# HGRN2 and short-convolution decoder step: 42 of 80 input projections as seven-product 2x2 block matrices, with stage results kept in DRAM

## The chip, the cores and the metric

The kernel runs on one core of one Trainium2 chip. The metric is the device time of one execution in microseconds (us); a smaller time is better. The engines are TensorE (PE, with its weight loads shown apart as PEld), VectorE (DVE), ScalarE (ACT), GpSimd (POOL) and SyncE (SP), which issues all the DMAs here.

## The reference

One decoder layer for 1040 prompt tokens (16 learned meta tokens, then 1024) and 8 single-token samples, width 1024, all in float32:

```python
xn = rmsnorm(h, norm_pre)
proj = xn @ w_in                         # 1024 x 10240: ten sections of 1024 channels
q, fr, i_in, z_a, b_g, c_g, h_c, z_b, gate_a, gate_b = split(proj)
f = lb + (1 - lb) * sigmoid(fr);  k = 1 - f;  qa = silu(q)
o = gated linear recurrence over (qa, k, i_in, log f), 8 heads of 128 x 128   # branch A
y_a = (rmsnorm(o) * silu(z_a)) @ w_a
u = c_g * h_c                                                                # branch B
y_b = (b_g * conv3(u) * silu(z_b)) @ w_b
out = (sigmoid(gate_a) * y_a + sigmoid(gate_b) * y_b) @ w_o
h = h + rmsnorm(out, norm_post)
```

The states of the recurrence and the last two rows of u are outputs too.

## The kernel before

**Layout.** Activations lie channel-major: 128 channels on the partitions, 1048 columns (NX) along the free dimension: even prompt chunks, odd prompt chunks back to front, 8 sample columns, 16 meta columns. The first 1032 (NY) have an output. The normalised input is eight such blocks, each split exactly into a high and a low float32r part (`xh`, `xl`), which stay in SBUF (tag `xn`) to the end.

**A section** is one block of 128 output channels of a projection. `weight` (L76) loads its 1024 x 128 weights (512 KB, line 79) and `split` (L89 to 92) makes the two parts: ACT casts the high part (L91), DVE subtracts it (L92). `gemm` (L94 to 105) then makes three matmuls for each of eight blocks k: high by high, high by low, low by high.

```python
94      def gemm(w, xh, xl, n0, n):
96          wh, wl = w
97          pt = gbank()
98          for k in range(8):
99              ks = slice(128 * k, 128 * k + 128)
100             pe.matmul(pt[:, 0:n], wh[:, ks], xh[k][:, n0:n0 + n], start=(k == 0), stop=False)
101             pe.matmul(pt[:, 0:n], wh[:, ks], xl[k][:, n0:n0 + n], start=False, stop=False)
102             pe.matmul(pt[:, 0:n], wl[:, ks], xh[k][:, n0:n0 + n], start=False, stop=(k == 7))
```

`section` (L107) runs it over three chunks of columns, 512, 256 and 264 to 280 wide (CH_Y, CH_C, CH_M, L127 to 129), 72 matmuls in all, and a function of the caller takes each chunk out of PSUM. There are 80 sections on the input (`w_sec`, eight for each of the ten parts of `proj`) and 16 on the outputs of the two branches (`w_a`, `w_b`).

**Order.** Head 0's four sections run by groups of columns while the input is still being normalised. For each of seven heads, `weave` (L531) puts the four sections of the next head (`projections`, L202) between the steps of one head's recurrence (`hgrn`, L209). Head 7's recurrence lies between four sections of gate A (L565). Then come the other gates A and y_a (L568), branch B (L588 to 634: for each m the sections 5, 6, 4 and 7, with u, the convolution and the products on DVE, ACT and POOL between them), gate B and y_b (L672 to 676, L717), and the output projection (L761), 512 columns to a matmul. The outputs of the branches and `merged` stay in SBUF (tag `z`, eight slots).

**What sets the order of the queues.** The tile framework fixes each engine's order when the program is built: by its own model of time it takes the first instruction in program order whose inputs and slots are ready. So a queue is not in program order (a weight cast is taken one section ahead), but on the chip each engine keeps to the order that was fixed. A tag has as many slots as its `bufs`; a new tile waits until the last reader of its slot is done. PSUM has four banks `g` and four banks `h`.

Of the kernel before, what the change touches and what calls it, by code (L numbers as in the profile page):

```python
# [19 lines left out]
NX = 1048  # L20
NY = 1032
# [9 lines left out]
def hybrid_step(ctx: ExitStack, tc: tile.TileContext,  # L31
# [41 lines left out]
    def small(n, tag="st", bufs=6):  # L73
        return sb.tile([128, n], F32, name=tag, tag=tag, bufs=bufs)

    def weight(src, raw=None, hi=None, lo=None, eng=None):  # L76
        """128 output channels of a [1024, *] weight: exact float32r parts [128, 8, 128]."""
        raw = slot(raw or "wr", 1024)
        sync.dma_start(raw.rearrange("p (k c) -> p k c", k=8), src.rearrange("(k p) c -> p k c", p=128))
        hi = slot(hi, 1024, F32R) if hi else slot("wh", 1024, F32R, 2)  # L80
        lo = slot(lo, 1024, F32R) if lo else slot("wl", 1024, F32R, 2)
        split(raw[:, 0:1024], hi[:, 0:1024], lo[:, 0:1024], eng)
        return hi, lo

    def w_sec(sec, m, *tags, eng=None):
        c0 = 1024 * sec + 128 * m
        return weight(w_in[0][:, c0:c0 + 128], *tags, eng=eng)
# [713 lines left out]
```

## Time and profile before

| what | value |
|---|---|
| runs | 1364.84 us median of 3 (1364.76 to 1364.93) |
| profiled execution, first to last instruction (span) | 1363.2 us |
| time of a run outside the span, by the median | 1.6 us |
| PE busy | 1341.0 us, 98% of the span, 8705 matmuls |
| DVE, ACT, POOL busy | 637.5, 347.8, 97.9 us |
| moved by DMA | 82.96 MB, 61 GB/s on average |

The profiled execution has no time of its own beside its span; the 1.6 us are the median of the runs less the span. Matmuls are pipelined, so the duration of one is longer than the distance to the next; what a matmul costs is read from the distance between starts.

### The profile page before, as it was taken

What the parts mean: (1) busy time and instruction counts of PE and PEld (TensorE: products, weight loads), DVE (VectorE), ACT (ScalarE), POOL (GpSimd) and SP (SyncE); (2) the same over time, 40 slices, a digit from 0 to 9 for tenths busy, and PEclk for the clock granted to TensorE, in tenths of its full rate; (3) what the DMA queues carried; (4) which work ended last, traced back from release to release, by engine and by line L of the source; (5) the groups of instructions that cost most, each with busy time, mean ns of one, the idle gap of its engine ahead of it and who ended that gap; (6) DMA issues with size and microseconds to landing.
All of it is one profiled execution on the core that took longest, in us unless ns stands there. A gap on an engine that the chain in (4) does not pass through costs nothing.

```text
span 1363.2 us, 20362 instructions
## 1 busy us (share of the span) xinstructions
PE 1341.0 (98%) x8705; PEld 1207.5 (89%) x8705; DVE 637.5 (47%) x1049; ACT 347.8 (26%) x702; POOL 97.9 (7%) x200
## 2 busy tenths in 40 slices
PE   6999999999999999999999999999999999999998
PEld 6989898989898999999999999999999999998786
DVE  5497676676767677521122333333333322216422
ACT  7233232323232333301111221122112211115211
POOL 5002010110101020100000000000000000000000
PEclk9999999999999999999999999999999999999999
DMA  7021312121221212111111111111111111123321
GB/s 235 19 63 50 87 33 86 34 78 50 63 78 51 62 49 63 34 47 47 47 47 47 47 47 47 47 47 47 47 47 47 49 47 47 47 62 110 112 98 70
DMA packets 125316, 82.96 MB, mean 61 GB/s; under 512 B 2911, under 2 KB 118728, under 8 KB 125226
## 3 DMA queue, kind: packets, MB, share of 16 engines
q1 hardware_dynamic: 125226, 81.67, 20.1%
q8 instruction: 68, 1.11, 0.3%
q14 instruction: 22, 0.18, 0.0%
HBM read 72.57 MB, written 9.05 MB: 60 GB/s over the span
## 4 chain that ended last, share of the span: by engine, by line
PE 91%; DVE 6%; DMA 1%; issue 1%; ACT 0%; POOL 0%; SPq 0%; DVEq 0%; POOLq 0%; ACTq 0%
PE g L100 25%; PE g L101 25%; PE g L102 25%; PE h L339 2%; PE g L771 2%; PE g L769 2%; PE g L770 2%; DVE a L347 2%; PE h L405 1%; PE h L404 1%; PE h L387 1%; DMA wr<-in_w_in_dram 1%; DVE x L342 1%; PE h L419 1%; PE h L370 1%
## 5 line engine op out<-in xcount | busy, mean ns | idle before, releaser
L100 PE MATMUL g<-xn,wh 128*128 128x256 f32 (+4 forms) x1888 | 613.3, 325 | 0.0
L101 PE MATMUL g<-xn,wh 128*128 128x256 f32 (+4 forms) x1888 | 603.6, 320 | 0.0
L102 PE MATMUL g<-xn,wl 128*128 128x256 f32 (+4 forms) x1888 | 603.5, 320 | 0.1
L100 PEld LDWEIGHTS g<-xn,wh 128*128 128x128 f32 x1888 | 356.8, 189 | 29.3 <-issue 1.6
L102 PEld LDWEIGHTS g<-xn,wl 128*128 128x128 f32 x1888 | 355.6, 188 | 27.5 <-DVE wl L92 0.5
L101 PEld LDWEIGHTS g<-xn,wh 128*128 128x128 f32 x1888 | 356.0, 189 | 26.6 <-DVE xn L92 0.2
L92 DVE TENSOR_TENSOR wl<-wr,wh 128x1024 fp32r<-128x1024 f32 x92 | 112.3, 1221 | 203.5 <-ACT wh L91 203.4
L91 ACT CAST wh<-wr 128x1024 fp32r<-128x1024 f32 x93 | 97.7, 1050 | 392.8 <-PE g L101 387.0
L347 DVE COPY_PREDICATED a<-masks,h 128x512 f32<-128x512 uint8 x56 | 59.4, 1061 | 4.3 <-PE h L335 4.1
L339 PE MATMUL h<-x,u 128*128 128x128 f32 x384 | 52.4, 279 | 4.5 <-DVE x L342 3.9
L339 PEld LDWEIGHTS h<-x,u 128*128 128x128 f32 x384 | 48.0, 191 | 8.3 <-issue 3.3
L337 ACT COPY u<-k 128x512 f32<-128x512 f32 x48 | 30.4, 632 | 90.5 <-DVE k L341 44.1
L597 DVE TENSOR_TENSOR u<-g,c 128x256 f32<-128x256 f32 (+2 forms) x32 | 12.9, 425 | 64.9 <-PE g L102 64.9
L557 DVE TENSOR_TENSOR z<-g,z 128x512 f32<-128x512 f32 (+2 forms) x24 | 12.4, 517 | 63.7 <-PE g L102 63.7
L342 DVE TENSOR_TENSOR x<-x,ee 128x512 f32<-128x512 f32 x48 | 33.0, 688 | 15.9 <-PE h L339 15.1
L743 DVE TENSOR_TENSOR z<-g,t 128x512 f32<-128x512 f32 x16 | 11.1, 691 | 57.0 <-ACT cs L742 57.0
L341 DVE TENSOR_TENSOR k<-k,ee 128x512 f32<-128x512 f32 x48 | 33.0, 688 | 4.8 <-ACT u L337 4.8
L621 DVE TENSOR_TENSOR t<-g,t 128x512 f32<-128x512 f32 (+2 forms) x24 | 12.4, 516 | 42.8 <-PE g L102 42.8
L101 PE MATMUL g<-zs,wh 128*128 128x512 f32 (+2 forms) x96 | 30.8, 321 | 0.0
L100 PE MATMUL g<-x,wh 128*128 128x512 f32 (+2 forms) x96 | 30.8, 320 | 0.0
L102 PE MATMUL g<-x,wl 128*128 128x512 f32 (+2 forms) x96 | 30.6, 319 | 0.0
L742 ACT ACTIVATE cs<-g 128x512 f32<-128x512 f32 x16 | 9.6, 597 | 74.8 <-PE g L771 45.4
(324 smaller groups left out, 1805.5 us busy)
## 6 DMA issues: line engine op xcount, KB each, us to landing
wr<-in_w_in_dram SPq DMA_DIRECT2D x77, 512.0 KB
z<-in_x_prompt_dram SPq DMA_DIRECT2D x8, 512.0 KB
sin<-in_state_hgrn_dram SPq DMA_DIRECT2D x8, 512.0 KB
vb<-vd SPq DMA_DIRECT2D x8, 512.0 KB
out_dram<-sin SPq DMA_DIRECT2D x8, 512.0 KB
wr<-in_w_a_dram SPq DMA_DIRECT2D x8, 512.0 KB
wr<-in_w_b_dram SPq DMA_DIRECT2D x8, 512.0 KB
out_dram<-z SPq DMA_DIRECT2D x16, 256.0 KB
```

The costliest lines, as they stand in the source:

```text
L91: act.copy(hi, src)
L92: (eng or vec).tensor_tensor(out=lo, in0=src, in1=hi.bitcast(F32), op=ALU.subtract)
L100: pe.matmul(pt[:, 0:n], wh[:, ks], xh[k][:, n0:n0 + n], start=(k == 0), stop=False)
L101: pe.matmul(pt[:, 0:n], wh[:, ks], xl[k][:, n0:n0 + n], start=False, stop=False)
L102: pe.matmul(pt[:, 0:n], wl[:, ks], xh[k][:, n0:n0 + n], start=False, stop=(k == 7))
L337: act.copy(comp(kms, ko, nb, B, B), kc)
L339: pe.matmul(pt[:, 128 * j:128 * j + 128], kms[:, ko + 128 * j:ko + 128 * j + 128], comp(X, 128 * j + B, nb // 4, 512 - B, B), start=True, ...
L341: vec.tensor_tensor(out=kc, in0=kc, in1=cap(eb, eo + 1, [[2, nb], [512 // B - 1, 2], [0, B]]), op=ALU.mult)
L342: vec.tensor_tensor(out=xc, in0=xc, in1=cap(eb, eo, [[2, nb], [512 // B + 1, 2], [0, B]]), op=ALU.mult)
L347: vec.copy_predicated(comp(A, B, nb, 512 - B, B), bass.AP(masks[:].tensor, masks[:].offset + 512 * l, ap=[list(masks[:].ap[0]), [2 * B, nb ...
L769: pe.matmul(pt, gh[k][:, ts], woh[k][:, hs], start=(k == 0), stop=False)
L770: pe.matmul(pt, gh[k][:, ts], wol[k][:, hs], start=False, stop=False)
```

## The change

The two halves of the columns are laid out alike, 524 wide (HL; 516, HY, have an output), and every chunk of a section is now 256 or 260 to 268 columns wide, four chunks for three. 38 of the sections on the input (all of the recurrence, gate A for m = 0 to 5) stay as they were otherwise. The other 42 (sections 5, 6, 4, 7 of branch B, gate A for 6 and 7, gate B) are taken in 21 pairs. A pair is a 2 x 2 block product (two blocks of output channels, two halves of the 1024 input channels, two halves of the columns), made by the seven products of Strassen's method in Winograd's form.

`block_sums` makes the four sums of the activations once: POOL adds the parts back together, DVE takes the differences, ACT and DVE split them. `strassen` makes four sums of weights for each pair on POOL and splits seven operands. The partial sums that more than one result needs are copied out of PSUM between products (`held`, slots `sc`, two of them). The outputs of the branches and the gates are stored to DRAM (`oz_d`, `ob_d`, `ga_d`, `gb_d`) and loaded again. The gates are all made before y_a and y_b. y_a, y_b and the first four blocks of the output projection take k as the outer loop. POOL takes part of branch B's products.

```diff
-    CH_M = ((0, 512), (512, 256), (768, 280))     # all columns
-    CH_Y = ((0, 512), (512, 256), (768, 264))     # prompt, sample
+    def halves(n):
+        return tuple((h, c0, w) for h in range(2) for c0, w in ((0, 256), (256, n - 256)))
+    CH_M = halves(HL)
+    CH_Y = halves(HY)
...
+    BUFS = {"x": 2, "f": 2, "k": 2, "zs": 2, "z": 2, "w": 6, "wr": 4, "cs": 2, "sc": 2, "st": 5}
...
     def run_hgrn(m):
+        Z = slot("z", NY)
         yield from hgrn(m, tiles[m], Z)
+        sync.dma_start(oz_d[m], Z)
...
-    weave(gates_first(), 24, run_hgrn(7), N_HG)
+    weave(gates_plain(0, 1, 2, 3), 32, run_hgrn(7), N_HG)
...
+    def block_sums():
+        for k in range(4):
+            ta, tb = (slot(t, 2 * HL) for t in (("kt", "s"), ("a", "ee"))[k % 2])
+            (r12, r22), (r11, r21) = ((t[:, 0:HL], t[:, HL:2 * HL]) for t in (ta, tb))
+            for r, b in ((r12, (0, 1)), (r11, (0, 0)), (r22, (1, 1)), (r21, (1, 0))):
+                h, l = in_block(blk[b])(k)
+                pool.tensor_tensor(out=r, in0=h.bitcast(F32), in1=l.bitcast(F32), op=ALU.add)
+            yield
+            d1 = t1_raw(k)
+            vec.tensor_tensor(out=d1, in0=r12, in1=r11, op=ALU.subtract)
+            vec.tensor_tensor(out=r12, in0=r22, in1=r12, op=ALU.subtract)
+            vec.tensor_tensor(out=r22, in0=r22, in1=d1, op=ALU.subtract)
+            split(r22, *in_quarters(t2)(k))
+            yield
+            vec.tensor_tensor(out=r21, in0=r21, in1=r22, op=ALU.subtract)
+            split(r12, *in_quarters(t3)(k))
+            yield
+            split(r21, *in_quarters(t4)(k))
+            yield
+
+    weave(gates_plain(4, 5), 16, block_sums(), 16)
+    bt = (slot("b01h", 4 * HL, F32R), slot("b01l", 4 * HL, F32R))
+    for k in range(4):
+        split(t1_raw(k), *in_block(bt)(k))
+    sets = [in_block(blk[0, 0]), in_block(blk[1, 0]), in_quarters(t2), in_block(bt), in_quarters(t3), in_quarters(t4),
+            in_block(blk[1, 1])]
...
+        def add(p):
+            if p < len(pairs):
+                sa, sb_ = (slot(t, 1024) for t in (("kt", "s"), ("a", "ee"))[p % 2])
+                s1, s2, s3, s4 = sums[p] = sa[:, 0:512], sa[:, 512:1024], sb_[:, 0:512], sb_[:, 512:1024]
+                pool.tensor_tensor(out=s1, in0=quad(p, 1, 0), in1=quad(p, 1, 1), op=ALU.add)
+                pool.tensor_tensor(out=s2, in0=s1, in1=quad(p, 0, 0), op=ALU.subtract)
+                pool.tensor_tensor(out=s3, in0=quad(p, 0, 0), in1=quad(p, 1, 0), op=ALU.subtract)
+                pool.tensor_tensor(out=s4, in0=quad(p, 0, 1), in1=s2, op=ALU.subtract)
+        def operand(i):
+            p, j = divmod(i, 7)
+            if p < len(pairs):
+                s1, s2, s3, s4 = sums[p]
+                src = (quad(p, 0, 0), quad(p, 0, 1), s2, s1, s3, quad(p, 1, 1), s4)[j]
+                w = ops[i] = slot("w", 1024, F32R)
+                split(src, w[:, 0:512], w[:, 512:1024])
...
+        for p, (_, chunks, evac, end) in enumerate(pairs):
+            b1, b2 = (gbank, hbank) if p % 2 == 0 else (hbank, gbank)
+            pa, pb, pc = ([b() for _ in chunks] for b in (b1, b2, b1))
+            for j in range(7):
+                i = 7 * p + j
+                if j == 0 and p:
+                    load(p + 1)
+                if j == 1:
+                    add(p + 1)
+                operand(i + 3)
+                w = ops.pop(i)
+                dst = (pa, pb, pa, pc, pa, pa, pc)[j]
+                for (c0, n), pt in zip(chunks, dst):
+                    for k in range(4):
+                        xh, xl = sets[j](k)
+                        mm3(pt[:, 0:n], w[:, 128 * k:128 * k + 128], w[:, 512 + 128 * k:640 + 128 * k],
+                            xh[:, c0:c0 + n], xl[:, c0:c0 + n], j in (0, 1, 3) and k == 0, k == 3,
+                            j not in (0, 1, 3))
+                if j in (0, 2, 4):
+                    sc = slot("sc", HL)
+                    for (c0, n), pt in zip(chunks, pa):
+                        act.copy(sc[:, c0:c0 + n], pt[:, 0:n])
+                    held[j] = sc
+                if j in (1, 4, 5, 6):
+                    r, h, banks, s = {1: (0, 0, pb, 0), 4: (1, 1, pc, 4), 5: (1, 0, pa, None), 6: (0, 1, pc, 2)}[j]
+                    for (c0, n), pt in zip(chunks, banks):
+                        evac(r, h, c0, n, pt[:, 0:n], None if s is None else held[s][:, c0:c0 + n])
+                if p == len(pairs) - 1 and j in tail:
+                    tail[j]()
+            end()
...
+    def b_pair(m):
+        def evac(r, h, c0, n, pt, s):
+            t = conv[m][:, HY * h + c0:HY * h + c0 + n]
+            if s is not None:
+                vec.tensor_tensor(out=s, in0=pt, in1=s, op=ALU.add)
+            y = pt if s is None else s
+            if r == 0:
+                (vec if h else pool).tensor_tensor(out=t, in0=t, in1=y, op=ALU.mult)
+            else:
+                sg = slot("cs", 512)[:, 0:n]
+                act.activation(out=sg, in_=y, func=AF.Sigmoid)
+                (pool if h else vec).tensor_tensor(out=sg, in0=y, in1=sg, op=ALU.mult)
+                vec.tensor_tensor(out=t, in0=t, in1=sg, op=ALU.mult)
+        return (sec_of(4, m), sec_of(7, m)), ((0, 256), (256, 260)), evac, lambda: sync.dma_start(ob_d[m], conv[m])
...
+    pairs = [f(m) for m in range(8) for f in (u_pair, b_pair)]
+    pairs.append(gate_pair(8, 6, ga_d))
+    pairs += [gate_pair(9, m, gb_d) for m in (0, 2, 4, 6)]
+    strassen(pairs, sets, tail)
...
+        for k in range(8):
+            ks = slice(128 * k, 128 * k + 128)
+            xh, xl = parts[k]
+            for (h, c0, n), pt in zip(CH_Y, banks):
+                o = HY * h + c0
+                mm3(pt[:, 0:n], wh[:, ks], wl[:, ks], xh[:, o:o + n], xl[:, o:o + n], k == 0, k == 7)
```

Of the parts left out: `mm3` is the three matmuls of `gemm`. `u_pair` takes sections 5 and 6 with chunks of 256 and 262 columns; its results of the first channel block go to C by a DVE add, those of the second are multiplied with C into u, for the first half of the columns on DVE and for the second on POOL (two instructions of 256 columns and a small one). At its end stand six small POOL copies, then for each half one ACT instruction and two DVE instructions of the convolution, 512 columns each, and three small ones on DVE. `gate_pair` ends in a sigmoid on ACT and two stores of 528 KB. `tail` loads branch A's output back and splits it into the slots of activation blocks that the last pair no longer reads.

## Rows read from the trace of the kernel before

**Rows 1.** The page: busy time of each engine, and PE, PEclk and GB/s by slices.

```profile
PE 1341.0 (98%) x8705; PEld 1207.5 (89%) x8705; DVE 637.5 (47%) x1049; ACT 347.8 (26%) x702; POOL 97.9 (7%) x200
...
PE   6999999999999999999999999999999999999998
...
PEclk9999999999999999999999999999999999999999
...
GB/s 235 19 63 50 87 33 86 34 78 50 63 78 51 62 49 63 34 47 47 47 47 47 47 47 47 47 47 47 47 47 47 49 47 47 47 62 110 112 98 70
```

**Rows 2.** The page: the chain that ended last, by engine.

```profile
PE 91%; DVE 6%; DMA 1%; issue 1%; ACT 0%; POOL 0%; SPq 0%; DVEq 0%; POOLq 0%; ACTq 0%
```

**Rows 3.** Windows: a head, branch B, the merge, 256-column matmuls alone.

```profile
core 0: us, PE busy (x) PEld busy (x) DVE busy (x) ACT busy (x) POOL busy (x), PEclk, DMA share, GB/s
...
260.00:400.00 140.00, 139.13 (x964) 126.75 (x963) 94.28 (x157) 43.52 (x101) 16.67 (x28) 1.00 0.20 58
...
960.00:1060.00 100.00, 100.00 (x631) 90.35 (x631) 36.99 (x64) 21.41 (x33) 2.12 (x14) 1.00 0.17 48
...
1160.00:1260.00 100.00, 99.91 (x640) 90.09 (x639) 36.96 (x57) 28.56 (x48) 0.00 (x0) 1.00 0.25 75
...
32.00:45.00 13.00, 13.00 (x110) 12.82 (x109) 6.62 (x12) 2.40 (x6) 1.70 (x2) 1.00 0.03 8
```

**Rows 4.** Timeline, PE: start, duration, line. First matmul of consecutive chunks in branch B.

```profile
778.47 0.28 PE L100 MATMUL g<-xn,wh 128*128 128x266 f32 x1
...
781.43 0.40 PE L100 MATMUL g<-xn,wh 128*128 128x512 f32 x1
...
787.03 0.28 PE L100 MATMUL g<-xn,wh 128*128 128x256 f32 x1
...
789.85 0.28 PE L100 MATMUL g<-xn,wh 128*128 128x264 f32 x1
...
792.78 0.40 PE L100 MATMUL g<-xn,wh 128*128 128x512 f32 x1
```

**Rows 5.** Groups by form, ACT: count, busy us, mean ns.

```profile
L91 ACT CAST c<-u 128x512 fp32r<-128x512 f32 x8 | 4.9, 613 | 4.2 <-DVE u L241 4.2
...
L590 ACT COPY c<-g 128x256 f32<-128x256 f32 x8 | 3.0, 372 | 17.9 <-PE g L102 17.9
```

**Rows 6.** The same view, DVE.

```profile
L613 DVE SCALAR_TENSOR_TENSOR t<-u,vecs,t 128x512 f32<-128x512 f32 x16 | 11.3, 746 | 0.0
...
L597 DVE TENSOR_TENSOR u<-g,c 128x256 f32<-128x256 f32 x16 | 6.8, 425 | 37.4 <-PE g L102 37.4
...
L92 DVE TENSOR_TENSOR c<-u,c 128x512 fp32r<-128x512 f32 x8 | 5.4, 677 | 0.0
```

**Rows 7.** Timeline, start of the kernel, POOL: a 1024-column subtraction.

```profile
13.64 2.38 POOL L92 TENSOR_TENSOR wl<-c,wh 128x1024 fp32r<-128x1024 f32 x1
```

**Rows 8.** The same stretch, DVE.

```profile
14.74 1.31 DVE L462 TENSOR_TENSOR lbt<-vecs 128x8 f32<-128x8 f32 x1
16.08 0.17 DVE L463 TENSOR_TENSOR lbt<-vecs,lbt 128x8 f32<-128x8 f32 x1
```

**Rows 9.** Timeline of a head, DVE and POOL.

```profile
166.25 0.67 DVE L341 TENSOR_TENSOR k<-k,ee 128x512 f32<-128x512 f32 x1
166.28 1.85 POOL L263 TENSOR_TENSOR k<-k,f 128x8 f32<-128x8 f32 x1
166.85 1.21 DVE L92 TENSOR_TENSOR wl<-wr,wh 128x1024 fp32r<-128x1024 f32 x1
168.21 0.76 POOL L263 TENSOR_TENSOR k<-k,em 128x8 f32<-128x8 f32 x3
```

**Rows 10.** Timeline, DVE: the end of head 7, and y_a's first chunk.

```profile
571.41 1.23 DVE L92 TENSOR_TENSOR s<-z,kt 128x1032 fp32r<-128x1032 f32 x1 [2.70 <-PE h L405]
...
582.20 0.69 DVE L557 TENSOR_TENSOR z<-g,z 128x512 f32<-128x512 f32 x1 [2.52 <-PE g L102]
```

**Rows 11.** The chain that ended last: wait for one 512 KB weight load.

```profile
62.85 3.60 DMA wr<-in_w_in_dram
```

More of the change, by code (lines that the diff above doesn't have):

```diff
@@ L15 @@
 EPS = 1e-6
-NX = 1048
-NY = 1032
+HL = 524
+HY = 516
+NX = 2 * HL
+NY = 2 * HY
 def cap(t, off, dims):
@@ L71, in rsqrt, with small @@
         pool.tensor_tensor(out=out, in0=out, in1=half[0:rows, 0:n], op=ALU.pow)
[L73 to L87, printed above, removed]
+    def small(n):
+        return slot("st", n)
     def split(src, hi, lo, eng=None):
@@ L565, in hybrid_step, with gate_plain @@
-    weave(gates_first(), 24, run_hgrn(7), N_HG)
-    for m in range(4, 8):
-        oz_parts(m)
-    for m in range(8):
-        if m >= 4:
-            drain(gate_a(m))
-        drain(y_a(m))
+        weave(projections(m + 1, tiles), 32, run_hgrn(m), N_HG, 1 if m else 2)
+    def gate_plain(m):
+        G = slot("z", NY)
+        yield from section(w_sec(8, m), CH_Y, lambda h, c0, n, pt: act.activation(
+            out=G[:, HY * h + c0:HY * h + c0 + n], in_=pt, func=AF.Sigmoid))
+        sync.dma_start(ga_d[m], G)
@@ new lines, in gate_pair, with evac, end @@
+    def gate_pair(sec, m, dst):
+        G = []
+        def evac(r, h, c0, n, pt, s):
+            if not G:
+                G.extend(slot("z", NY) for _ in range(2))
+            if s is not None:
+                vec.tensor_tensor(out=s, in0=pt, in1=s, op=ALU.add)
+            act.activation(out=G[r][:, HY * h + c0:HY * h + c0 + n], in_=pt if s is None else s, func=AF.Sigmoid)
+        def end():
+            for r in range(2):
+                sync.dma_start(dst[m + r], G[r])
+        return (sec_of(sec, m), sec_of(sec, m + 1)), ((0, 256), (256, 260)), evac, end
@@ new lines, in fill @@
+    def fill(src, parts, ks, places):
+        raws = {}
+        for k in ks:
+            raws[k] = slot(("c", "u", "t")[k % 3], NY)
+            sync.dma_start(raws[k], src[k])
+        his, los = places
+        for k, hi, lo in zip(ks, his, los):
+            split(raws[k][:, 0:NY], hi, lo)
+            parts[k] = hi, lo
+    pa, pb = {}, {}
+    one = lambda *tags: [place(t, 1)[0] for t in tags]
+    tail = {0: lambda: fill(oz_d, pa, (0, 1), (place("b00h", 2), place("b00l", 2))),
+            1: lambda: fill(oz_d, pa, (2, 3), (place("b10h", 2), place("b10l", 2))),
+            2: lambda: fill(oz_d, pa, (4, 5), (one("x", "k"), one("f", "zs"))),
+            3: lambda: fill(oz_d, pa, (6, 7), (place("b01h", 2), place("b01l", 2)))}
@@ L646, in w_bm, with gate_in, w_am @@
+    def gate_in(src, m):
+        g = slot("z", NY)
+        sync.dma_start(g, src[m])
+        return g
+    def w_am(m):
+        return weight(w_a[0][:, 128 * m:128 * m + 128])
     def w_bm(m):
         return weight(w_b[0][:, 128 * m:128 * m + 128])
[L649 to L658 removed]
@@ new lines, in hybrid_step, with ev @@
+    for m in range(8):
+        w, g = wb, gb
+        if m < 7:
+            wb, gb = w_bm(m + 1), gate_in(gb_d, m + 1)
+        def ev(ys, pt):
+            vec.tensor_tensor(out=g[:, ys], in0=pt, in1=g[:, ys], op=ALU.mult)
+            vec.tensor_tensor(out=merged[m][:, ys], in0=merged[m][:, ys], in1=g[:, ys], op=ALU.add)
+        y_gemm(w, pb, ev)
+        if m == 2:
+            out_weight(0, *one("x", "f"))
+            out_weight(1, *one("k", "zs"))
+        if m == 4:
+            (h2, h3), (l2, l3) = place("b01h", 2), place("b01l", 2)
+            out_weight(2, h2, l2)
+            out_weight(3, h3, l3)
+        if m == 5:
+            merged_parts(0, *one("c", "u"))
```

551 lines of the change are left out of this document (290 added, 261 removed).

## Prediction

> **What bounds the kernel now.** I read the page first, then the chain, the windows, and the starts of single matmuls. TensorE is busy in 98% of the span and, but for the first and the last slice, in all slices at nine tenths or more, at full granted clock [rows 1]. The chain that ended last is 91% PE [rows 2]. By stages: inside the heads PE is idle for 0.87 of 140 us, in branch B for nothing, in the merge for 0.09 of 100 us [rows 3]. So time goes only where matmul time goes, and stays only where nothing new makes PE wait. In branch B DVE is busy 37% of the time, ACT 21%, POOL 2%: there is room beside PE, but a change that fills it must be checked for waits.
>
> What a matmul costs is the distance between starts: a chunk of 24 takes 5.60 us at 512 columns, 2.82 us at 256, 2.93 us at 264, 2.96 us at 266 [rows 4], which is 233, 117.5, 122 and 123 ns. A matmul of 256 columns thus costs half of one of 512; per further column it costs (122 - 117.5)/8, some 0.55 ns, so that I take 120 ns for 260 columns, 121 for 262 and 124 for 268.
>
> **Part 1, seven products for eight.** A pair before is two sections. Of branch B's sections 5 and 6: 2 x (5.60 + 2.82 + 2.96) = 22.8 us; of all the others: 2 x (5.60 + 2.82 + 2.93) = 22.7 us. A pair after is 7 products x 4 blocks k x 3 matmuls = 84 matmuls on each of two chunks: 84 x (0.1175 + 0.121) = 20.0 us, and 84 x (0.1175 + 0.120) = 19.95 us. One product is a seventh, 2.86 us. The gain is 8 x 2.75 + 13 x 2.75 = **58 us**, all of it on the path.
>
> Does a stream of 256-column matmuls alone keep this pace? In the stretch from 32 to 45 us there is nearly nothing else, and 110 records in 13 us are one in 118 ns [rows 3]. The Trainium skill (TensorE: Matmul & The Clock Gate, section Back-to-back issue gap) speaks against the change here: it has streams of weight load and matmul sustain 131 ns at 512 columns and 81 ns at 128, so that fewer columns save far less than in proportion. An estimate on the line between these two is 98 ns at 256; by it a pair would go from 48 x (131 + 98 + 98) ns = 15.7 us to 168 x 98 ns = 16.5 us, and the change would lose 17 us instead of gaining 58. The trace does not agree: 233 and 117.5 ns.
>
> **Part 2, four chunks for three.** The plain sections and y_a, y_b: 24 x (0.1175 + 0.120) x 2 = 11.40 us against 11.35; for 28 sections of heads 1 to 7, 6 of gate A and 16 of y_a and y_b that is **+2 us**. Head 0 had four chunks before.
>
> **Part 3, the sums of the activations.** Here I expect a stall. POOL's price is not shown at this size: 2.38 us for 1024 columns [rows 7] makes 1.19 for 512 and 1.22 for 524. A DVE subtraction of 512 with both inputs in SBUF takes 0.677 us [rows 6], 0.69 for 524. These two do not run side by side: while POOL's 2.38 us instruction ran, a DVE instruction on 8 columns, 0.17 us otherwise, took 1.31 us and ended with it [rows 7, 8]; and POOL's 0.2 us instruction took 1.85 us behind two DVE instructions one right after the other, to the end of the second [rows 9]. So the times add: `block_sums` has 16 POOL adds, 19.5 us, and 4 x (4 + 3) DVE instructions, 19.3 us. POOL can begin when head 7's slots come free, at 571.4 [rows 10], and ends the first four adds near 576.3. Three rounds of 4.9 + 4.8 us follow, to 605.4, then 3.4 us (four DVE instructions and a cast) until the last quarter of the third product's operand: 608.8. PE's cover: gates 0 to 3 end at 582.2 - 5.6 = 576.6 (y_a's first chunk is taken out at 582.2 [rows 10]), gates 4 and 5 take 22.8 us, the first two products need no sum, 5.7 us: 605.1. The stall is some 4 us, and about 4 more because POOL's sums for the first pairs and the split of the fourth operand (4 x 0.69 us) compete for the same time: **8 us**. Bounds: 0 if the order that is built lets the sums begin earlier, 15 if no product goes ahead of them: 605.4 + 4.8 + 2.8 + 1.3 for a first operand, against 599.4.
>
> **Part 4, the work beside a pair.** Of a u pair in its 20 us: POOL 4 sums at 1.19, two products at 0.6, a small one and six copies at 0.25 [rows 9]: 7.7 us. DVE with two SBUF inputs: 7 x 0.677 + 4 x 0.746 + three small, 8.3 us; these two exclude each other, 16 of 20 us. DVE's instructions on PSUM add 8 x 0.425 = 3.4 us [rows 6]. ACT: 7 casts at 0.613, 6 copies at 0.372 [rows 5], two of 512 at about 0.61: 7.8 us. A b pair has 7.2 and 7.3 us in place of 7.7 and 8.3. So each engine fits behind PE, the shared path at 80%. Waits by place: the operands are made up to five products ahead (six slots `w`), 14 us, which covers any queue seen here. The copies of `pa` must be done before the next product onto `pa`; after the first and third product another lies between (2.86 us), after the fifth only the half product of the other chunk, 1.43 us, against a cast that may be in front and the copy, 0.613 + 0.372. The DVE adds on `pc` have 2.86 us, against one POOL sum that may be in front, a split and two adds: 1.19 + 0.677 + 2 x 0.425 = 2.7. Both just fit. A trace of these waits does not exist; bounds are 0 and one late instruction (a POOL sum, 1.2 us) at each of the two tight places in 21 pairs, 50 us. I take 0.3 us per pair, **6 us**, near the low end, since each place has its cover even with one instruction in front.
>
> SP: a b pair's store of 528 KB waits for the last product, some 2 us into the next pair, and two loads of 512 KB are queued behind it. One load takes 3.6 us and more [rows 11]; 1.55 MB at the 235 GB/s of the first slice [rows 1] are 6.6 us. They land near 9 us, and the first cast from them is needed at the latest at 11 us if it is taken three products ahead: nothing on the path. The y stages move 1.04 MB in 11.4 us, 91 GB/s, less than the 112 of the last slices.
>
> **Part 5, the rest.** In the heads each section has one more evacuation, each head two more POOL instructions and one more small DMA: PE covers them, idle 0.6% there. If that cover were gone, an evacuation would cost its 0.37 us. Two `z` slots for eight make a gate wait for the store of the one before the last; four PSUM banks, 2.85 us of matmuls each, stand before that. The splits of branch A's output fall in the last pair, 8 x 1.2 us of DVE in 20, where no next operands are made. The merge and the output projection keep their matmuls. Together **+4 us**, between 0 and 10.
>
> **Sum.** 1363.2 - 58 + 2 + 8 + 6 + 4 = 1325.2 us of span, and with the 1.6 us outside it (median 1364.84 less 1363.2) **1327 us**.
>
> **The rivals.** (a) *No stalls*: the order that is built hides parts 3 to 5. For it: PE's 98% now. 1363.2 - 58 + 2 + 1.6 = 1309 us. (b) *POOL and DVE hold up PE*: the two exclude each other and 80% is near the limit, so evacuations come late. Part 3 at 15 us, parts 4 and 5 at 20 and 8: 1352 us. For it: POOL waited through two DVE instructions, alike in six of the eight heads [rows 9]; against it: five products of lead. (c) *Slower: the copies of partial sums come late on ScalarE.* Place: `held` before products three, five and six of a pair. ACT keeps to an order fixed in advance; if a sigmoid or a cast in front of the copy waits for a DVE instruction that waits for POOL (1.2 + 0.7 us), PE stops each time. It decides from (58 - 2 - 8 - 4)/21 = 2.1 us per pair; at 1.2 us in each of three places, 3.6 us per pair, the time is 1327 - 6 + 76 = 1397 us. For it: three waits of PE that were not there before, in each pair; against it: ACT has 12 of 20 us free. (d) *Seven products save nothing*: 256-column matmuls met one after another for 400 us cost 133 ns instead of 117.5, or the stalls happen to equal the gain: within 2.7 us of 1365. Only the stretch of 13 us speaks on it, and against it.
>
> **How the numbers follow.** Forecast 0.48, (a) 0.17, (b) 0.16, (c) 0.15, (d) 0.04. About 0.2% is what a measurement of this kernel can tell from no change. Forecast, (a) and (b) are faster, 0.81; (d) is the same, 0.04; (c) is slower, 0.15. The range of the forecast itself is 1313 to 1345 (its unknown terms from some 4 to 36 us); the range for eight in ten takes in (a) at its lower end and (b) with 8 us to spare at its upper, 1309 to 1360, and leaves out (c) and (d).
>
> **What would show it.** Chunks of 24 matmuls at 256 columns still 2.82 us; a pair some 20 us from start to start, with PE idle below 0.5 us in it; one gap of PE of 5 to 10 us behind gate A's sixth section, ended by DVE or ACT; DVE subtractions stretched to over 1 us wherever POOL's sums run. I would be wrong if pairs are 21.5 us or longer, with PE waiting for ACT's copies or DVE's adds, if the gap behind the gates is 15 us, or if heads or y stages, where I expect nothing, become longer by more than 1%.

## The result, and the profile after

| | before | after |
|---|---|---|
| median of the runs | 1364.88 us (1364.76 to 1365.02, 4 runs) | 1324.52 us (1323.37 to 1328.36, 4 runs) |
| profiled execution, span | 1363.2 us | 1322.1 us (the run: 1323.88) |
| PE busy | 1341.0 us, 8705 matmuls | 1293.5 us, 10409 matmuls |
| DVE, ACT, POOL busy | 637.5, 347.8, 97.9 us | 771.5, 433.0, 295.2 us |
| bytes moved | 82.96 MB | 117.07 MB |

The ratio of the times is 0.971, with a 95% interval of 0.9695 to 0.9723: faster by 40 us. The forecast was 1327 us.

The page of the kernel after: the busy times, PE by slices, and the chain by engine, which answer to [rows 1, 2].

```profile
PE 1293.5 (98%) x10409; PEld 1259.5 (95%) x10409; DVE 771.5 (58%) x1336; ACT 433.0 (33%) x959; POOL 295.2 (22%) x372
...
PE   6999999999999999998999999999999999999997
...
PE 90%; DVE 6%; POOL 1%; DMA 1%; ACT 1%; issue 1%; SPq 0%; DVEq 0%; POOLq 0%; ACTq 0%
```

PE is still what bounds the kernel. One new slice in the middle has an 8: it lies near 600 us, where the pairs begin. The windows answer to [rows 3]. The columns are the window, its length, the busy time and number of instructions of PE, PEld, DVE, ACT and POOL, then the granted clock, the DMA share and GB/s. First come 5 us near the start of the pairs, then a u pair, a b pair, and 100 us of pairs.

```profile
609.00:614.00 5.00, 3.97 (x21) 3.97 (x21) 5.00 (x6) 3.55 (x8) 3.05 (x3) 0.66 0.36 105
...
652.37:672.56 20.19, 20.19 (x170) 20.19 (x169) 10.37 (x23) 6.30 (x13) 6.97 (x7) 1.00 0.27 80
672.56:692.55 19.99, 19.99 (x170) 19.99 (x169) 12.95 (x23) 8.81 (x19) 10.99 (x13) 1.00 0.18 54
...
700.00:800.00 100.00, 100.00 (x837) 100.00 (x837) 60.12 (x109) 37.64 (x79) 44.54 (x53) 1.00 0.22 64
```

**A pair in the steady state has no wait at all.** PE is busy for 20.19 of 20.19 us and for 19.99 of 19.99. The starts of the first matmul of each of the 21 pairs, taken from PE's timeline, lie 28.16 us apart at the first pair, 21.01 at the second, 20.19 (u pairs) or 19.97 to 20.00 (b and gate pairs) at the next 18, and 21.49 from the last pair to the first matmul of y_a. The timeline of PE in one u pair, first matmul of consecutive chunks, answers to [rows 4]:

```profile
772.92 0.28 PE L109 MATMUL g<-b00h,w 128*128 128x256 f32 x1
...
774.34 0.28 PE L109 MATMUL g<-b00h,w 128*128 128x262 f32 x1
...
775.79 0.28 PE L109 MATMUL h<-b10h,w 128*128 128x256 f32 x1
...
777.20 0.28 PE L109 MATMUL h<-b10h,w 128*128 128x262 f32 x1
```

Twelve matmuls take 1.42 us at 256 columns and 1.45 us at 262, that is 118 and 121 ns each, for 117.5 and 121 forecast.

**What the start of the pairs costs.** The timeline of PE at the first pair:

```profile
604.61 0.28 PE L111 MATMUL g<-b00h,w 128*128 128x256 f32 x1
610.03 0.58 PE L109 MATMUL g<-b00h,w 128*128 128x262 f32 x1 [5.15 <-ACT z L564]
610.42 0.42 PE L110 MATMUL g<-b00l,w 128*128 128x262 f32 x1
...
612.60 0.42 PE L111 MATMUL g<-b00h,w 128*128 128x262 f32 x1
...
613.52 0.29 PE L110 MATMUL h<-b10l,w 128*128 128x256 f32 x1
```

PE stands still for 5.15 us, until ACT has taken gate 5's second chunk (a sigmoid) out of the bank that the second half of product one needs. Then the eleven matmuls from 610.42 to 612.60 start 0.218 us apart, where the same shape takes 0.121 elsewhere. The granted clock of the 5 us from 609 is 0.66 on average, so PE ran at its lower level of 1.2 GHz for most of them; some 15 matmuls at 0.1 us more are 1.5 us. The Trainium skill (TensorE: Matmul & The Clock Gate, section Back-to-back issue gap) gives columns divided by 1.2 as the gap in ns of a single matmul at the lower clock. An estimate by this formula for 262 columns is 218 ns, and the trace agrees.

Why was the sigmoid late? ACT's timeline, then DVE's and POOL's, in the same stretch:

```profile
591.24 0.39 ACT L564 ACTIVATE z<-g 128x260 f32<-128x260 f32 x1 [2.48 <-PE g L111]
600.93 1.17 ACT L85 CAST f<-kt 128x524 fp32r<-128x524 f32 x2 [9.31 <-DVE kt L597]
...
606.83 0.62 ACT L85 CAST w<-kt 128x512 fp32r<-128x512 f32 x1 [3.76 <-POOL kt L629]
...
609.07 0.63 ACT L85 CAST f<-a 128x524 fp32r<-128x524 f32 x1 [0.56 <-DVE a L597]
609.60 0.38 ACT L564 ACTIVATE z<-g 128x260 f32<-128x260 f32 x1
```

```profile
580.36 0.69 DVE L595 TENSOR_TENSOR c<-kt,s 128x524 f32<-128x524 f32 x1
...
592.17 1.79 DVE L595 TENSOR_TENSOR u<-kt,s 128x524 f32<-128x524 f32 x1 [3.74 <-POOL s L592]
593.89 1.80 DVE L86 TENSOR_TENSOR sin<-ee,it 128x524 fp32r<-128x524 f32 x1
...
607.27 1.76 DVE L597 TENSOR_TENSOR a<-a,u 128x524 f32<-128x524 f32 x1
```

```profile
586.04 3.56 POOL L592 TENSOR_TENSOR kt<-b01h,b01l 128x524 f32<-128x524 f32 x1 [7.95 <-DVE k L86]
589.56 1.31 POOL L592 TENSOR_TENSOR kt<-b11h,b11l 128x524 f32<-128x524 f32 x1
...
595.09 1.77 POOL L592 TENSOR_TENSOR a<-b11h,b11l 128x524 f32<-128x524 f32 x1
596.83 1.78 POOL L592 TENSOR_TENSOR ee<-b00h,b00l 128x524 f32<-128x524 f32 x1
```

The sigmoid at 609.60 stands in ACT's fixed order behind casts that wait: one of the block sums for 9.31 us for DVE, one of the first pair's weight sums for 3.76 us for POOL, and the last one, at 609.07, for the difference that DVE ends at 609.03. DVE and POOL take turns from 592 to 600 us, when POOL adds the block sums, and again from 603.9 us on, when it makes the weight sums (L628 to 631) of the first pair. A DVE instruction that takes 0.69 us alone is on record for 1.8 us, a POOL add that takes 1.31 us alone for 1.77; one of each starts every 1.72 us, a little less than the 2.0 us that the two would take one after the other. The Trainium skill (SBUF — State Buffer, section SBUF: two separate sides) calls this an exclusive lock between a GpSimd instruction and a VectorE instruction with two SBUF inputs; taking turns in the trace agrees with it. Two waits for slots come before that: DVE's first difference waits for the slot of head 7's output until 580.36, and POOL waits 7.95 us for a slot that DVE's splits have to free.

### The profile page after: what moved, and what is told of

The parts are those of the page before. It is cut to its first block, busy times and chain, and to the rows that moved or that the text cites. A ratio compares the mean times of both kernels' runs of the same rounds, so it can differ in the third digit from the quotient of the medians.

```text
span 1322.1 us, 24885 instructions
## 1 busy us (share of the span) xinstructions
PE 1293.5 (98%) x10409; PEld 1259.5 (95%) x10409; DVE 771.5 (58%) x1336; ACT 433.0 (33%) x959; POOL 295.2 (22%) x372
## 2 busy tenths in 40 slices
DMA packets 134590, 117.07 MB, mean 89 GB/s; under 512 B 3953, under 2 KB 119770, under 8 KB 134478
## 4 chain that ended last, share of the span: by engine, by line
PE 90%; DVE 6%; POOL 1%; DMA 1%; ACT 1%; issue 1%; SPq 0%; DVEq 0%; POOLq 0%; ACTq 0%
PE g L109 19%; PE g L110 18%; PE g L111 18%; PE h L111 8%; PE h L110 8%; PE h L109 8%; PE h L366 3%; PE h L433 1%; PE h L431 1%; PE h L414 1%; DVE w L86 1%; PE h L171 1%; PE h L447 1%; PE h L397 1%; DMA it<-in_x_prompt_dram 0%
## 5 line engine op out<-in xcount | busy, mean ns | idle before, releaser
L86 DVE TENSOR_TENSOR w<-wr,w 128x512 fp32r<-128x512 f32 (+1 forms) x114 | 127.0, 1115 | 58.5 <-ACT w L85 58.5
L109 PE MATMUL g<-b00h,w 128*128 128x256 f32 (+1 forms) x448 | 131.8, 296 | 5.5 <-ACT z L564 5.1
L110 PE MATMUL g<-b00l,w 128*128 128x256 f32 (+1 forms) x448 | 128.2, 286 | 0.0
L111 PE MATMUL g<-b00h,w 128*128 128x256 f32 (+1 forms) x448 | 128.0, 286 | 0.0
L109 PE MATMUL g<-b10h,w 128*128 128x256 f32 (+2 forms) x440 | 125.8, 286 | 0.0
L110 PE MATMUL g<-b10l,w 128*128 128x256 f32 (+2 forms) x440 | 124.7, 283 | 0.0
L111 PE MATMUL g<-b10h,w 128*128 128x256 f32 (+2 forms) x440 | 124.4, 283 | 0.0
L109 PE MATMUL g<-b01h,w 128*128 128x256 f32 (+3 forms) x416 | 119.4, 287 | 0.0
L110 PE MATMUL g<-b01l,w 128*128 128x256 f32 (+3 forms) x416 | 117.9, 283 | 0.2 <-DVE b01l L86 0.2
L111 PE MATMUL g<-b01h,w 128*128 128x256 f32 (+3 forms) x416 | 117.8, 283 | 0.0
L109 PE MATMUL g<-b11h,w 128*128 128x256 f32 (+3 forms) x384 | 112.1, 292 | 0.0
L111 PE MATMUL g<-b11h,w 128*128 128x256 f32 (+3 forms) x384 | 108.7, 283 | 0.0
L109 PEld LDWEIGHTS g<-b00h,w 128*128 128x128 f32 x448 | 86.0, 193 | 8.8 <-ACT z L564 5.4
L111 PEld LDWEIGHTS g<-b00h,w 128*128 128x128 f32 x448 | 86.0, 192 | 0.0
L109 PEld LDWEIGHTS g<-b10h,w 128*128 128x128 f32 x440 | 83.0, 189 | 0.4 <-issue 0.2
L111 PEld LDWEIGHTS g<-b10h,w 128*128 128x128 f32 x440 | 82.9, 188 | 0.0
```

Source lines behind the costliest of these rows:

```text
L109: pe.matmul(pt, wh, xh, start=first, stop=False, skip_group_check=onto)
L110: pe.matmul(pt, wh, xl, start=False, stop=False, skip_group_check=onto)
L111: pe.matmul(pt, wl, xh, start=False, stop=last, skip_group_check=onto)
```

## The experiments

The question after the result: is the gain the missing product alone, does the sharing of the block sums between DVE and POOL make the stall, and how far are the pairs from the tight places that the prediction named? Each run is compared with runs of the kernel before on the same chip.

| run | median us | ratio to before, 95% interval | first pair | steady u, b pairs |
|---|---|---|---|---|
| after | 1324.52 | 0.9695 to 0.9723 | 28.16 | 20.19, 19.99 |
| e1 eight products | 1379.72 | 1.0087 to 1.0117 | | 23.1 (mean) |
| e2 last sums on DVE | 1327.12 | 0.9707 to 0.9736 | 29.99 | 20.19, 20.0 |
| e3 weight sums twice | 1369.42 | 1.0017 to 1.0043 | 35.4 | 20.2 to 21.6, 22.2 to 24.1 |
| e4 other slot first | 1328.66 | 0.9720 to 0.9752 | 20.29 | 20.19, 20.0 |
| e5 first pair's sums early | 1322.84 | 0.9670 to 0.9705 | 22.25 | 20.19, 20.0 |
| e6 all sums on DVE | 1318.10 | 0.9647 to 0.9680 | 20.48 | 20.19, 20.0 |
| e7 weight sums on DVE | 1323.50 | 0.9684 to 0.9716 | 26.41 | 20.19, 19.99 |
| e8 six sums | 1333.07 | 0.9747 to 0.9780 | 32.28 | 20.19, 19.99 to 20.9 |
| e9 e6 without the early sums | 1320.38 | 0.9659 to 0.9693 | 21.25 | 20.19, 20.0 |
| e10 e6 with the old slot order | 1321.04 | 0.9661 to 0.9693 | 23.76 | 20.19, 20.0 |

The last two columns are distances between starts in the trace, in us. The last one leaves out the first two pairs; "20.19, 20.0" stands for pairs as in the kernel after, single b pairs up to 0.7 us longer.

**e1: eight products in the same order, layout and spilling.** A pair is again two sections of eight blocks k, in four chunks each. The block sums, the weight sums and the copies of partial sums go; everything else of the change stays.

```diff
-    weave(gates_plain(4, 5), 16, block_sums(), 16)
+    drain(gates_plain(4, 5))
...
-    strassen(pairs, sets, tail)
+    eight(pairs)
```

> The 21 pairs as plain products (eight for seven), with the chunks, stores, order of the stages and the rest of the changed kernel; no block sums. Theory (the gain is the missing product): 96 matmuls on each chunk at the distances of the changed kernel, 118.3, 119.6 and 122 ns for 256, 260 and 262 columns, are 22.8 and 23.1 us a pair, 481 us in all where the changed kernel takes 432 for this stage: 1324.5 + 49 = about 1373 us, and no gap before the first pair. Rival (the gain comes from the new order of stages and the looser buffers, the products only fill time): below 1335 us.

1379.72 us, 1% slower than before and 7 us above the 1373 expected. The window of its start of the pairs shows no wait:

```profile
600.00:640.00 40.00, 40.00 (x337) 39.83 (x336) 8.71 (x15) 7.84 (x15) 6.62 (x18) 1.00 0.17 54
```

From 605.4 us to y_a's first matmul at 1089.9 its 21 pairs take 484.5 us, 23.07 each. So the change without its saved products, and without the sums that these need, costs 15 us. Some 7 of them come from the smaller chunks: a pair of plain sections takes 23.07 us in four and took 22.72 in three (30 sections of branch B before lie 11.36 us apart on average). The saved products, less all that their sums cost, are worth 1379.7 - 1324.5 = 55 us. The spans of the two traces are 56.3 us apart; 52.6 of these lie in the stage of the pairs (484.5 us for 431.9), and most of the rest before it.

**e2: the adds of the last two quarters on DVE.**

```diff
-                pool.tensor_tensor(out=r, in0=h.bitcast(F32), in1=l.bitcast(F32), op=ALU.add)
+                (vec if k > 1 else pool).tensor_tensor(out=r, in0=h.bitcast(F32), in1=l.bitcast(F32), op=ALU.add)
```

> In block_sums the eight adds of k = 2 and 3 on DVE in place of POOL. Theory (POOL and DVE exclude each other when both read two SBUF operands): eight adds cost the shared path 8 x 1.31 us on POOL and 8 x 0.69 us on DVE, so the sums end some 5 us earlier and the stall of about 9 us at the first two pairs shrinks by as much: about 1319.5 us, and DVE's differences take 0.69 us there, not 1.8. Rival (the two run side by side and DVE is slow for another reason): DVE has 5.5 us more to do before the first pair, about 1330 us.

1327.12 us; the stall did not shrink. DVE's differences did take 0.70 us, but PE waited elsewhere. PE's timeline, then POOL's, ACT's and DVE's:

```profile
616.13 0.58 PE L111 MATMUL g<-x,w 128*128 128x256 f32 x1 [6.00 <-DVE w L86]
```

```profile
596.93 5.35 POOL L628 TENSOR_TENSOR kt<-wr 128x512 f32<-128x512 f32 x1 [19.01 <-DVE zs L86]
602.36 1.27 POOL L629 TENSOR_TENSOR kt<-kt,wr 128x512 f32<-128x512 f32 x1
```

```profile
603.66 1.14 ACT L85 CAST w<-kt 128x512 fp32r<-128x512 f32 x2 [6.48 <-POOL kt L629]
```

```profile
611.84 3.44 DVE L86 TENSOR_TENSOR b01l<-u,b01h 128x524 fp32r<-128x524 f32 x2
...
615.41 1.28 DVE L86 TENSOR_TENSOR w<-kt,w 128x512 fp32r<-128x512 f32 x2
```

The first pair's weight sums wait 19.01 us for a slot of the block sums. The first of them, 1.3 us alone, then stays on record for 5.35 us beside an unbroken row of DVE instructions. That is not yet what PE waits for: the sum of product three is done at 603.6 us and cast by 604.8. Its split on DVE starts at 615.41 only, since in DVE's fixed order it stands behind the splits of the fourth operand (`b01l`), and these take turns with POOL's weight sums for the second pair. Moving an add to DVE does not cure anything by itself if the order that is then built puts such work in front of an operand.

**e3: the four weight sums of each pair twice on POOL.** The sums are computed twice over, to the same slots, with the same values.

```diff
-                pool.tensor_tensor(out=s1, in0=quad(p, 1, 0), in1=quad(p, 1, 1), op=ALU.add)
+                for _ in range(2):
+                    pool.tensor_tensor(out=s1, in0=quad(p, 1, 0), in1=quad(p, 1, 1), op=ALU.add)
...
```

> Each of POOL's four sums of weights of a pair is made twice, to the same place. Theory (exclusive): a u pair has POOL 8 x 1.29 + 3.3 = 13.6 us and DVE 8.3 us with two SBUF operands, 21.9 of 20.2 us; a b pair 13.3 + 7.3 = 20.6 of 20.0; a gate pair 15. The u and b pairs become 0.6 to 2 us longer, in all 10 to 25 us: 1335 to 1350 us. Rival (side by side): POOL is busy 13.6 of 20 us and DVE 12, both fit behind PE: 1324 us, within 3.

1369.42 us: the rival, side by side at 1324, is out, and the effect is larger than the 10 to 25 us expected. PE's waits (total, times, longest), and DVE's and PE's timeline at one of them:

```profile
PE h L109 <- DVE sc L753: 15.5, 8, 2.4
PE g L109 <- ACT z L564: 9.6, 1, 9.6
PE h L109 <- ACT sc L671: 7.7, 4, 4.3
PE g L109 <- ACT sc L671: 4.0, 2, 2.2
```

```profile
709.40 0.43 DVE L761 TENSOR_TENSOR t<-t,cs 128x256 f32<-128x256 f32 x1 [5.19 <-POOL cs L760]
709.74 0.42 DVE L753 TENSOR_TENSOR sc<-h,sc 128x260 f32<-128x260 f32 x1
```

```profile
710.22 0.39 PE L109 MATMUL h<-b11h,w 128*128 128x260 f32 x1 [1.85 <-DVE sc L753]
```

These are the two places of Part 4: the DVE adds on `pc` (L753, once in each of the eight b pairs) and the copies of `pa` (L671). They show how it happens. Not DVE's own length makes the add late: in front of it in DVE's fixed order stands a product (L761) that waits 5.19 us for a product on POOL (L760), which stands behind the doubled sums. But this does not show the exclusion by itself. In front of this wait POOL works without a break from 695.55 to 708.64 us, most of its sums take 1.3 us there and two 1.75, and DVE is idle at the end; so the doubling adds some 5 us to POOL's own row, whatever DVE does. After several of the gaps PE also runs at its lower clock: from 700 to 800 us the granted clock is 0.97 where it was 1.00.

**e4: the slot that comes free first is taken first for the differences.**

```diff
-    t1 = [slot(t, 2 * HL) for t in ("c", "u")]
+    t1 = [slot(t, 2 * HL) for t in ("u", "c")]
```

> The differences d1 of block_sums take slot u for k = 0, 1 and slot c for k = 2, 3, the other way round; c holds head 7's output until 580 us, u is free some 20 us earlier. Theory (the gap of 5.4 us at the first pair is the late start of DVE's differences at 580.4 us, with POOL's and DVE's times added up behind it): the differences of k = 0 and 1 start before 570 us, the gap and the slow clock behind it go, 7 to 9 us: about 1316.5 us. Rival (the gap comes from ScalarE's fixed order or the z slots, whatever DVE does): no change, 1324 us within 2.

1328.66 us, outside both. The differences do begin near 573 us and the first pair takes 20.29 us, but the wait now lies inside gate 5, which takes 19.19 us for 12.16. PE's timeline:

```profile
602.56 0.39 PE L109 MATMUL g<-b01h,w 128*128 128x256 f32 x1 [4.22 <-ACT z L564]
...
607.97 0.39 PE L109 MATMUL g<-b01h,w 128*128 128x260 f32 x1 [0.78 <-ACT z L564]
```

ACT's sigmoids stand behind casts that wait for DVE, which takes turns with POOL, as before; beginning earlier only brings this forward. Of the 2.8 us by which its span is longer than that of the kernel after, 1.8 lie in the last pair (23.3 us for 21.49), where the wait is that of e10 below.

**e5: e2, and two of the first pair's weight sums made before the block sums, in the slot `t`.**

```diff
+    first = [load_weight(sec_of(5, 0)), load_weight(sec_of(6, 0))]
+    first_s = slot("t", 1024)
...
+    pool.tensor_tensor(out=first_s[:, 0:512], in0=q0(1, 0), in1=q0(1, 1), op=ALU.add)
+    pool.tensor_tensor(out=first_s[:, 512:1024], in0=first_s[:, 0:512], in1=q0(0, 0), op=ALU.subtract)
     weave(gates_plain(4, 5), 16, block_sums(), 16)
...
```

The small transposes of the convolution's state, which use the slot `t` too, move ahead of these lines.

> This is the kernel of the run with the last two quarters' adds on VectorE, with two of the first pair's four weight sums made before the block sums, in a slot of their own. Theory: the 6.0 us wait of that run at product three was GpSimd's first weight sum, which waited for a slot and then was passed over; with the sums ready the wait falls under 1.5 us, the first pair is at most 25 us and the time about 1321 us (1327.1 less 5 to 6). Rival: any shortage at the start shows up at the next place, since VectorE has the same number of instructions to do before product five; then a wait of 4 us or more stands at another operand and the time is 1325 to 1328 us.

1322.84 us, between the two theories. The 6.0 us wait is gone, and a smaller one of 1.75 us stands in its place. PE's timeline, ACT's, and POOL's:

```profile
614.94 0.39 PE L109 MATMUL g<-x,w 128*128 128x262 f32 x1 [1.75 <-ACT sc L681]
```

```profile
613.48 0.62 ACT L85 CAST w<-kt 128x512 fp32r<-128x512 f32 x1 [3.43 <-POOL kt L644]
614.00 0.61 ACT L85 CAST w<-wr 128x512 fp32r<-128x512 f32 x1
614.52 0.37 ACT L681 COPY sc<-g 128x262 f32<-128x262 f32 x1
```

```profile
601.99 11.46 POOL L644 TENSOR_TENSOR kt<-wr 128x512 f32<-128x512 f32 x1 [11.09 <-DVE zs L86]
```

The copy of `pa` stands on ACT behind a cast of the third weight sum, and that sum stays on record for 11.46 us on POOL, through a row of DVE instructions.

**e6: all sixteen adds on DVE, e4's order of the slots, e5's early sums.**

```diff
-                pool.tensor_tensor(out=r, in0=h.bitcast(F32), in1=l.bitcast(F32), op=ALU.add)
+                vec.tensor_tensor(out=r, in0=h.bitcast(F32), in1=l.bitcast(F32), op=ALU.add)
...
-    t1 = [slot(t, 2 * HL) for t in ("c", "u")]
+    t1 = [slot(t, 2 * HL) for t in ("u", "c")]
...
+    first_s = slot("t", 1024)
...
```

> All sixteen adds of the block sums on VectorE at 0.69 us, the slots taken in the order in which they come free, and the first pair's two sums early. Theory: what stalls at the start is the alternation of VectorE and GpSimd at 1.8 us each; 44 instructions of 0.69 us are 30 us from about 570, under the cover of gates 4 and 5 and of two products. No gap over 1 us between 560 and 640 us, the first pair at most 21.5 us, the time 1315 to 1318 us, the 9 us of the start gone. Rival: the adds stand in front of head 7's last steps on VectorE's queue and push them back, or ScalarE's sigmoids still stand behind casts that wait for VectorE; then 3 to 8 us of waits appear before the first pair, and the time stays at 1321 us or above.

1318.10 us, at the upper edge of what the theory expected; the first pair takes 20.48 us. The window of the start, DVE's row of instructions and the one POOL sum in it:

```profile
600.00:640.00 40.00, 39.39 (x327) 38.98 (x326) 30.63 (x43) 17.21 (x36) 29.66 (x24) 1.00 0.27 80
```

```profile
597.92 0.69 DVE L595 TENSOR_TENSOR c<-a,ee 128x524 f32<-128x524 f32 x1
598.54 0.68 DVE L86 TENSOR_TENSOR w<-wr,w 128x512 fp32r<-128x512 f32 x1
599.14 0.70 DVE L596 TENSOR_TENSOR a<-a 128x524 f32<-128x524 f32 x1
```

```profile
596.85 9.01 POOL L644 TENSOR_TENSOR kt<-wr 128x512 f32<-128x512 f32 x1 [6.17 <-DVE zs L86]
```

DVE's instructions are back at 0.69 us and PE's clock at 1.00. Its interval, up to 0.9680, lies below that of the kernel after, from 0.9695: this version beats both kernels.

**e9 and e10: e6 without its early sums, and e6 with the old order of the slots.** The first diff is e9 against e6, the second e10 against e6.

```diff
...
-    first_s = slot("t", 1024)
...
```

```diff
-    t1 = [slot(t, 2 * HL) for t in ("u", "c")]
+    t1 = [slot(t, 2 * HL) for t in ("c", "u")]
```

> The run with all sums on VectorE, without its second part: the first pair's weight sums are made after the block sums again. Theory: in that run a GpSimd sum that met VectorE's unbroken row of 0.69 us instructions took 9.01 us, and it was harmless because the two sums that product three needs had been made before; without them product three waits 4 to 8 us for its operand, as it did (6.0 us) in the run with half the adds on VectorE: 1322 to 1326 us, first pair 25 to 29 us. Rival: all that mattered was to keep GpSimd off the block sums; then the first pair stays under 22 us and the time is 1318 us within 2.

> The run with all sums on VectorE, without its third part: the differences go into the slot of head 7's output first again, so that they begin near 580 us and not near 572. Theory: from 580 us some 36 of the 44 instructions are left, 25 us; product three needs the 41st near 605 us and begins at 610, so that the order of the slots is worth nothing by itself: first pair at most 22 us, 1317 to 1321 us. Rival: the 8 us later start is what the cover lacks: a wait of 3 us or more in the first pair, 1322 us or above.

e9: 1320.38 us, first pair 21.25 us. The theory of the starved sum falls here. POOL's first weight sum does take 5.31 us, as in e2, but PE's largest wait in the first pair is 0.2 us. The difference to e2 is DVE's order; here the splits of product three's operand stand in front of those of the fourth operand, the first of them at 606.62:

```profile
606.62 0.68 DVE L86 TENSOR_TENSOR w<-kt,w 128x512 fp32r<-128x512 f32 x1
```

The rival is right about the pair, and its time is 0.4 us outside what it allowed. e10: 1321.04 us with a first pair of 23.76 us: the theory's 22 us are exceeded, by the same wait as in e5 (1.76 us for the copy of `pa`). In this run's trace the last pair takes 24.65 us, for 21.41 in e6. There PE waits 2.11 us for a copy of `pa`, which stands on ACT behind a cast of branch A's output, and this cast waits for its load from DRAM:

```profile
1024.05 1.05 ACT L85 CAST x<-u 128x1032 fp32r<-128x1032 f32 x1 [3.06 <-DMA u<-oz]
```

In the kernel after the same cast waits 1.49 us and PE 0.46. The intervals of e6, e9 and e10 overlap, so what each of the two smaller parts is worth stays open. What the three have in common, no POOL add in the block sums, is what takes the long wait away. Whether it is the turns, the shorter add (0.69 us on DVE for 1.31 on POOL) or the order that is then built, these runs do not tell apart.

**e7: the pairs' weight sums on DVE.**

```diff
-                pool.tensor_tensor(out=s1, in0=quad(p, 1, 0), in1=quad(p, 1, 1), op=ALU.add)
+                vec.tensor_tensor(out=s1, in0=quad(p, 1, 0), in1=quad(p, 1, 1), op=ALU.add)
...
```

> The four weight sums of each pair on VectorE in place of GpSimd (0.68 us each for 1.29 us). Theory: no engine beside PE is near its limit inside a pair, so the pairs stay at 20.19 and 19.99 us, and only the start can change, by up to 4 us either way: 1320 to 1328 us. Rival: that nothing waits in a pair depends on GpSimd taking the sums; VectorE's queue then makes the adds onto the last bank late, at least 0.3 us in every pair, and the time is 1330 us or more.

1323.50 us, with pairs of 20.19 and 19.99 us. The window of 100 us of pairs, with DVE at 68%:

```profile
700.00:800.00 100.00, 100.00 (x838) 100.00 (x837) 68.21 (x129) 37.96 (x79) 19.17 (x33) 1.00 0.22 64
```

Which of the two engines makes the sums is all one in a steady pair.

**e8: six sums in place of four.** The first two, s1 and s2, are computed twice, as in e3.

```diff
+                for _ in range(2):
+                    pool.tensor_tensor(out=s1, in0=quad(p, 1, 0), in1=quad(p, 1, 1), op=ALU.add)
+                for _ in range(2):
+                    pool.tensor_tensor(out=s2, in0=s1, in1=quad(p, 0, 0), op=ALU.subtract)
```

> The first two of a pair's four weight sums are made twice on GpSimd: six sums a pair, between the kernel after (four, no wait in the pairs) and the run with eight (b pairs 22.5 to 24.1 us). Theory: it is a matter of the time that GpSimd and VectorE with two SBUF inputs need one after the other; by Part 4 that is 16 us of 20 with four sums, 18.6 with six and 21.2 with eight in a u pair, 17.1 and 19.7 in a b pair, so that six still fit: steady pairs at most 20.4 us, waits only in the first two, 1326 to 1333 us in all. Rival: what counts is how much stands in front at the two tight places, the copies after product five and the adds onto pc; each further sum costs the same, the b pairs are 1 to 2 us longer throughout, and the time is 1338 to 1350 us, halfway to the run with eight.

1333.07 us, at the theory's upper edge. The first two pairs take 32.28 and 23.39 us; of the later ones before the gate pairs all but two are within 20.4, the two at 20.74 and 20.93. After the second pair PE stops only twice for half a microsecond or more, by 0.5 and 0.7 us. Eight sums cost 45 us more than four; six cost 9, of which 6.5 lie in the first two pairs. So the pairs go over an edge between six and eight sums; they do not get longer with each sum. Whether the time that POOL and DVE share sets this edge, or POOL's own row (e3), is not shown.

## Why the prediction was right

**Part 1 (gain of 58 us): right, 55.7 measured.** In the trace before, the starts of 31 consecutive sections of branch B lie 340.8 us apart, 11.36 us each, so 42 sections took 477.1 us; 8 x 20.19 + 13 x 19.99 are 421.4. The rest to 58 is mostly in the pairs after, 20.07 us on average for 19.97. The 55 us of e1 are another quantity: against eight products in the same small chunks the pairs save 484.5 - 421.4 = 63 us, from which the waits and what stands at the pairs' two ends take back 10.5. The spacing at 256 columns held for 430 us, 118 ns for 117.5; the estimate from the Trainium skill (TensorE: Matmul & The Clock Gate, section Back-to-back issue gap) that spoke against the change, 98 ns, is not borne out by the trace.

**Parts 2 and 5 (2 and 4 us): 4.9 together.** The span fell by 41.1. The pairs at the two ends lost 8.0, 1.0 and 1.5 us, but 0.8 of the last are small transposes of the convolution's state, which the kernel before makes too. So 55.7 - 9.7 = 46.0 leaves 4.9 for the heads, gates 0 to 5, the y stages and the output. The sections of y_a and y_b take 11.45 and 11.49 us for 11.35 before, 0.9% and 1.2% more, where 11.40 was forecast; in all these are some 2 us. For y_b it is just over the 1% that the prediction named as a sign of being wrong. Moving 41% more bytes shows at one place only, in the last pair (Part 4).

**Part 3 (a stall of 8 us): the size right at 8.0, the way only in part.** The first pair took 28.16 - 20.19 = 8.0 us more than a u pair. Right was that POOL's and DVE's times nearly add up (1.72 us for one of each, 2.0 by the sum) and that the gap stands behind gate A's sixth section. Three steps were not as forecast. The adds began at 563.96, not at 571.4, but the differences had to wait for the slot of head 7's output, until 580.36, and POOL then waited for a slot until 586.04; I had both begin with the first slots that came free and go on without a break. The wait was not for the third product's operand but for a sigmoid on ACT, two products earlier: I counted the sums' work on POOL and DVE and left out what stands behind their casts on ACT. And 1.5 us are a lower clock after the gap, which I did not count at all. That the size came out has some luck in it: an earlier wait, and a lower clock, in place of a longer one later. e4 shows that an earlier start of the differences alone gains nothing; e6, e9 and e10 show that it is the adds on POOL beside DVE's row that make the long wait.

**Part 4 (6 us): mis-sized; 0 in the steady pairs, 1.0 in the second and 0.7 in the last.** I took 0.3 us for each pair without a row that showed such waits. The two waits of the kernel after lie at the first tight place, the copy after product five:

```profile
646.58 0.38 PE L109 MATMUL h<-it,w 128*128 128x256 f32 x1 [0.79 <-ACT sc L667]
...
1028.43 0.38 PE L109 MATMUL g<-it,w 128*128 128x256 f32 x1 [0.46 <-ACT sc L667]
```

In the last pair the copy stands on ACT behind the cast that waits for branch A's output from DRAM (e10), which the prediction counted as work on DVE alone. e3 shows PE waiting at both tight places; but with the four sums of the change each keeps enough cover in a steady pair. The share of 80% for the path that DVE and POOL share was the better guide: by the same sum six sums make 93% of a u pair, and the pairs hold (e8); eight make 106%, and b pairs, where the sum is 98%, lose 2.2 us and more (e3). With the 1.29 us that a sum of weights takes on POOL, for the 1.19 forecast, these are 96%, 108% and 103%. That the b pairs lost more than the u pairs is not what this sum says; there DVE waits for a product on POOL in the middle of its queue.

**The sum.** The span came out 3.1 us under the forecast of 1325.2: the gain 2.3 us smaller, and parts 2 and 5, 3 and 4 together 5.4 us cheaper (14.6 for 20). So errors of either sign cancel in it.

**The rivals.** (a), no stalls, is what e6 comes nearest to, with 1318 us for 1309: the gain is 2.3 us smaller, parts 2 and 5 cost some 4 us that (a) did not have, and 2.4 are small waits in the pairs. (b) and (c) do not hold for the change, but their mechanism is what e3 brings about with twice the sums: copies late on ACT 11.7 us and adds late on DVE 15.5 us in all. (d) falls with the spacing of 118 ns.

## What to carry to other kernels

When products are saved by adding sums on other engines, look at two places apart: the steady loop, where here six sums, some 93 to 96% of PE's time on the two engines that exclude each other, still cost next to nothing and eight did not, and the start, where sums that all products need are made in a row. There, follow each engine's fixed order: what is late is not the sum's reader but whatever stands behind it in a queue (here a sigmoid that frees a PSUM bank). Here such a row of sums was best given to one engine of the excluding pair; shared between the two (the kernel after, e2), it left a wait of 5 to 6 us, and where they took turns it made the instructions of both longer.

## What was not expected of the hardware

Taking turns is not the only way in which DVE and POOL meet. In the kernel after, from 592 us on, each instruction of one lets one of the other through (1.8 and 1.77 us). But one POOL sum of 1.3 us stayed on record for 5.35, 9.01 and 11.46 us (e2, e6, e5), and a POOL add of the kernel after, at 586.04, for 3.56, while DVE went through instruction after instruction at 0.69 us with no loss. In all four the POOL instruction ends some 1.2 us after the end of DVE's row. What decides between the two was not tried. And a gap of PE costs more than its length: after 5.15 us without work, 1.5 us more went to matmuls at the lower clock (0.218 us for 0.121).
